# Eighteen product matmuls walk their columns in plain order, and nine separate contiguous matmuls are taken out

## The chip, the cores and the metric

The kernel runs on one core of a Trainium2 chip. The metric is the device time of one execution in microseconds. TensorE does the matrix products, VectorE, ScalarE and GpSimd the elementwise work, and DMA queues bring the weights from HBM. In rows of the profile PE is TensorE's matmul, PEld its weight load, DVE is VectorE, ACT ScalarE, POOL GpSimd, SP the engine whose queue issues the weight loads.

## The reference, cut to what matters

One layer of a hybrid decoder on 256 prompt tokens and 8 x 8 sample tokens (320 columns in all), model width 2048, feed-forward width 5632, in float32:

```python
xn = rms_norm(x, g_mix)
z = xn @ w_in                        # [B | C | h | q | k | v | gate_conv | gate_attn]
u = c_gate * h_conv
conv_out, conv_state = short_conv(u, conv_prev, w_conv)
y_conv = (b_gate * conv_out) @ w_conv_out
attn = prompt_attention(...)         # or sample_attention, window 128, sinks
y_attn = attn @ w_attn_out
merged = sigmoid(gate_c) * y_conv + sigmoid(gate_a) * y_attn
h = x + merged @ w_o
hn = rms_norm(h, g_ffn)
h = h + (silu(hn @ w_gate) * (hn @ w_up)) @ w_down
```

The output is the final norm of h, the last keys and values, and the convolution's state.

## The kernel before, in words

Activations lie with features on the 128 partitions and the 320 tokens along the free axis. Every float32 operand is held in two parts, hi and lo, in TensorE's rounded format, and a product of a weight block of 128 x 128 with the activations is three matmuls of 320 columns: hi x hi (pass 0), hi x lo (pass 1) and lo x hi (pass 2). `passes` (L150) orders them: passes 0 and 1 of a block follow one another and pass 2 comes some blocks later.

A product for 256 output features is `product` (L172): for each chunk of four blocks of 128 input features, `load_cols` (L132) issues the weights' DMA on SP's queue, ACT rounds them to `whi` (L129), DVE takes the rest as `wlo` (L130), and TensorE runs 24 matmuls of 320 columns (L186). Keys and values have a loop of their own, `kv_product` (L346, matmul at L372), whose chunks are four of one block and then six of two. The layer's order is: kv, q, then four times C, H, B, then eight times gc, ga, yc, ya, then eight wo (L186 each), then two halves of gate and up products (fg, fu) with the down product (dn, L997 to L1005) behind each half.

An activation row of 320 columns is stored as five pieces of 64 columns, 1040 elements apart for `xh`, `xl`, `hh` and `hl`. A product's matmul reads it, and writes its PSUM tile, in the order of `turns` (L101): four columns of piece 0, four of piece 1, and so on to piece 4, then the next four of each. The weights are read in plain order.

Between the chunks, `tick` (L145) advances a generator of side work: attention. Its matmuls stand on TensorE between chunks of C, H and B: eight visits for the prompt's scores (`prompt_scores`, L551, tiles `ps`), two for its values (`po`, L629), one for the sample's scores (`pss`, L689) and one for its values (`spo`, L753 and L763). In the first gate product's wake, two matmuls with ones (L211) give the second norm.

At nine places the kernel before has an additional matmul, `nudge` (L205). Its output is a scratch PSUM tile that nobody reads; it multiplies 320 neighbouring columns of `xh` (or `hh`) with 128 neighbouring columns of `xl` (or `hl`), in plain order:

```python
def nudge(rows, weights, n=T):
    x, w = (bass.AP(r.tensor, r.offset, [list(r.ap[0]), [1, m]]) for r, m in ((rows(0), n), (weights(0), P)))
    nc.tensor.matmul(ps_aux(u("nudge"))[:, :n], w, x, start=True, stop=True)
```

The places are: ahead of block 6 of kv; ahead of the third q product; behind the last of the eight visits of the prompt's scores; behind both visits of its values; behind the sample's scores; behind the sample's values; and ahead of the first up product of each half.

Of the kernel before, what the change touches and what calls it, by code (L numbers as in the profile page):

```python
# [17 lines left out]
T = TP + NB * TS  # L18
# [8 lines left out]
P = 128  # L27
# [25 lines left out]
def hybrid_layer(ctx: ExitStack, tc: tile.TileContext, a: dict, o: list):  # L53
    nc = tc.nc
# [17 lines left out]
    def ps_aux(name):  # L72
        return aux[0].tile([P, 512], F32, tag="aux", name=name)
# [3 lines left out]
    def u(s):  # L77
        uid[0] += 1
        return f"{s}_{uid[0]}"
# [21 lines left out]
    def turns(ap):  # L101

        return ap.rearrange("p s (i b) -> p i s b", b=4)

    def fives(ap):

        return ap.rearrange("p (s j) -> p s j", s=NS)
# [24 lines left out]
    def load_cols(w, k0, n, c0, behind=()):  # L132
# [4 lines left out]
            split_to(hi[:, :n, :], lo[:, :n, :], raw[:, :n, :])  # L137
        return hi, lo

    mark = {}  # L140
    side_work = [None]
    pending = []
    last = {}
# [28 lines left out]
    def product(load, nk, xh, xl, name, tiles=None, loaded=None):  # L172

        ps = [ps_acc(u(name)) for _ in range(2)]
        k0 = 0
        for n in tiles or [min(KT, nk - k) for k in range(0, nk, KT)]:
            hi, lo = load(k0, n)
            if loaded:
                loaded()
            order = [(k, c) for k in range(n) for c in range(2)]  # L180
            if k0 + n == nk:
                order.sort(key=lambda kc: kc[1])
            for k, c, i in passes(order, k0 + n == nk):
                kc = k0 + k
                w, x = ((hi, xh), (hi, xl), (lo, xh))[i]
                last["mm"] = nc.tensor.matmul(  # L186
                    turns(fives(ps[c][:, :T])), w[:, k, c * P:(c + 1) * P], turns(x(kc)),
                    start=(kc == 0 and i == 0), stop=(kc == nk - 1 and i == 2),
                )
            k0 += n  # L190
            while pending:
                with after(last["lo"], last["mm"]):
                    pending.pop(0)()
            tick()
        return ps

    def two_parts(src, tags=("ta", "tb")):
# [3 lines left out]
        nc.scalar.activation(hi, src, AF.Copy)  # L201
        nc.vector.tensor_sub(lo, src, hi.bitcast(F32))
        return hi, lo

    def nudge(rows, weights, n=T):  # L205
        x, w = (bass.AP(r.tensor, r.offset, [list(r.ap[0]), [1, m]]) for r, m in ((rows(0), n), (weights(0), P)))
        nc.tensor.matmul(ps_aux(u("nudge"))[:, :n], w, x, start=True, stop=True)

    def over_partitions(out, parts):
        for i, x in enumerate(parts):  # L210
# [48 lines left out]
    xh, xl = row_tiles(xp, ("xh_t", "xl_t"), KC, LEAD_X, ("xh", "xl"))  # L259
# [26 lines left out]
    def x_load(i, eng=nc.sync):  # L286
# [11 lines left out]
        out=ident, in_=ident, compare_op=ALU.not_equal, fill=1.0, base=0, pattern=[[-1, P]],  # L298
# [47 lines left out]
    def kv_product(tiles, x_after):  # L346

        ps = [ps_acc(u("kv")) for _ in range(4)]
        k0 = 0
        x_prep(0)  # L350
        for i, n in enumerate(tiles):
            if k0 == 6:
                nudge(xh, xl)
            hi, lo = load_kv(k0, n)
            if i == 0:
                x_prep(1)
            for b in x_after.get(i, ()):
                x_load(b)
            order = [(k, c) for k in range(n) for c in range(4)]
            if k0 + n == KC:  # L360
                order.sort(key=lambda kc: kc[1])
            seq = passes(order, k0 + n == KC)
            if i == 0:
                seq.sort(key=lambda kcm: kcm[2])
            for k, c, m in seq:
                kc = k0 + k
                if k0 and (k, c, m) == (0, 3 if n > 1 else 1, 0) and k0 + n < KC:
                    for kk in range(tiles[i + 1]):
                        x_prep(k0 + n + kk)
                    tick()  # L370
                w, x = ((hi, xh), (hi, xl), (lo, xh))[m]
                last["mm"] = nc.tensor.matmul(  # L372
                    turns(fives(ps[c][:, :T])), w[:, k, c * P:(c + 1) * P], turns(x(kc)),
                    start=(kc == 0 and m == 0), stop=(kc == KC - 1 and m == 2),
                )
            k0 += n
            if i == 0:
                tick()
        return ps
# [88 lines left out]
    def at_rows(part):  # L468
# [15 lines left out]
        out=sides[:, 0], in_=sides[:, 0], compare_op=ALU.is_ge, fill=0.0, base=-1, pattern=[[-1, WIN]],  # L484
# [158 lines left out]
    def prompt_attention():  # L643
        units = [(j * 2 + par, gp) for j in range(2) for gp in range(2) for par in range(2)]
        bias, sc, sm, turned, pts = {}, {}, {}, {}, {}
        bias[0] = bias_load(*units[0])
        for i in range(len(units) + 3):
            if i < len(units):
                if i + 1 < len(units):
                    bias[i + 1] = bias_load(*units[i + 1])  # L650
                sc[i] = prompt_scores(*units[i], bias.pop(i))
                if i + 1 == len(units):
                    nudge(xh, xl)
                yield
                sm[i] = prompt_softmax(*units[i], sc[i])
            if 0 <= i - 3 < len(units):
                pts[i - 3] = prompt_sides(i - 3, turned.pop(i - 3))
            yield
            if i >= 4 and i % 4 == 2:
                for n in (i - 5, i - 3):  # L660
                    kv, gp = units[n]
                    prompt_pv(kv // 2, gp, (pts.pop(n - 1), pts.pop(n)))
                nudge(xh, xl)
            if 0 <= i - 1 < len(units):
                turned[i - 1] = prompt_norm(i - 1, sc.pop(i - 1), *sm.pop(i - 1))
            yield
# [3 lines left out]
    def sample_attention(sm):  # L670
# [10 lines left out]
        for base in range(0, NB, 3):  # L681
            ps = ps_aux(u("pss"))
            n = min(3, NB - base)
            for b in range(base, base + n):
                o0 = (b - base) * W2
                for kv in range(NKV):
                    j, par = kv // 2, kv % 2
                    rows = slice(par * 64, par * 64 + 64)
                    nc.tensor.matmul(  # L689
                        ps[kv * 32:(kv + 1) * 32, o0:o0 + W2], qs[rows, j, b, :], kf[rows, b, j, :],  # L690
                        start=True, stop=True,
# [2 lines left out]
                s[:, base:base + n, :], ps[:, 0:n * W2].rearrange("p (b k) -> p b k", b=n),  # L694
                flip(bias_s).unsqueeze(1).to_broadcast([P, n, W2]),
            )
        nudge(xh, xl)
        yield
        yield

# [49 lines left out]
        for j in range(2):  # L750
            for par in range(2):
# [4 lines left out]
                    start=True, stop=False,  # L756
                )
        for b in range(NB):
            cv = cvs.pop(b)
            for j in range(2):  # L760
                for par in range(2):
# [3 lines left out]
                        cv[:, kv * HD:(kv + 1) * HD], ptw[:, kv, b * 32:(b + 1) * 32],  # L765
                        start=False, stop=(b == NB - 1),
                    )
        nudge(xh, xl)
        yield
        for j in range(2):  # L770
            src = pos[j][:, 0:256].rearrange("p (b g t) -> p g b t", b=NB, g=GRP)
            o = LEAD_A + j * 4 * at_row
            rows = at_t[:, o:o + 4 * at_row].rearrange("p (g w) -> p g w", g=GRP)[:, :, -2 * JS:]
# [42 lines left out]
    for j in range(2):  # L816
        for gp in range(2):
            if (j, gp) == (1, 0):
                nudge(xh, xl)
            ps = in_pair(O_Q + (j * 2 + gp) * CW, "q")  # L820
            pending.append(lambda j=j, gp=gp, ps=ps: q_out(j, gp, ps))
    side_work[0] = attention()
# [2 lines left out]
    for cp in range(4):  # L825
        c_sb = []
        ps = in_pair(O_C + cp * CW, "C")
# [4 lines left out]
        ps = in_pair(O_H + cp * CW, "H")  # L832
        conv = []
        for c in range(2):
# [13 lines left out]
            n = UL - 2  # L848
# [10 lines left out]
        ps = in_pair(O_B + cp * CW, "B")  # L859
# [17 lines left out]
    mm = mp_.enter_context(tc.tile_pool(name="mm", bufs=1, side="right"))  # L877
# [9 lines left out]
    for mp in range(8):  # L887
        c0 = mp * CW
        sg = {}
        for nm, off, tag in (("gc", O_GC, "ta"), ("ga", O_GA, "tb")):  # L890
            ps = in_pair(off + c0, nm)
# [5 lines left out]
        ps = product(  # L897
            lambda k0, n: load_cols(w_co, k0, n, c0), 8,
            cv_h, cv_l, "yc",
        )  # L900
# [126 lines left out]
    for half in range(2):  # L1027
# [4 lines left out]
        for fpair in range(nf // 2):  # L1032
            c0 = (f0 + fpair * 2) * P
            psg = product(
                lambda k0, n: load_cols(w_g, k0, n, c0), KC,
                hh, hl, "fg",
            )
            if half == 0 and fpair == 0:
                pss = ps_aux("pss2")
                over_partitions(pss[:, :T], two_parts(hacc, ("tc", "td")))  # L1040
                rstd_of(pss[:, :T], [P, T], "r2", hp, out=rb2)
            gs = []
            for c in range(2):
                t, t2 = tmp("ta", "gs")[:, :T], tmp("tb", "sg")[:, :T]
                nc.vector.tensor_mul(t, psg[c][:, :T], rb2)
                last["sig"] = nc.scalar.activation(t2, t, AF.Sigmoid)
                nc.vector.tensor_mul(t, t, t2)
                nc.vector.tensor_mul(t, t, rb2)
                gs.append(t)
            if fpair == 0:  # L1050
                nudge(hh, hl)
            psu = product(
                lambda k0, n: load_cols(w_u, k0, n, c0), KC,
                hh, hl, "fu",
            )
            for c in range(2):
                nc.vector.tensor_mul(gs[c], psu[c][:, :T], gs[c])
                f = fpair * 2 + c
                (first, rest), row = parts_of(gs[c]), a_move(f)
                nc.scalar.activation(row[:, :, JR:JT], rest, AF.Copy)  # L1060
                last["hi"] = nc.scalar.activation(row[:, :, 0:JR], first, AF.Copy)
                nc.vector.tensor_sub(row[:, :, JT:], rest, row[:, :, JR:JT].bitcast(F32))
                last["lo"] = nc.vector.tensor_sub(placed(a_low(f)), first, row[:, :, 0:JR].bitcast(F32))
                if half == 1:
                    nc.scalar.activation(a_first(f), gs[c][:, 0:P], AF.Copy)
# [258 lines left out]
```

## Time and profile before

| what | value |
|---|---|
| time, median of 3 runs | 1593.38 us (1593.12 to 1593.64) |
| time of the profiled execution | 1593.85 us |
| its span, first to last instruction | 1592.1 us |
| PE busy | 1583.2 us (99% of the span), 10899 matmuls |
| PEld busy | 1547.1 us (97%) |
| DVE busy | 890.9 us (56%) |
| ACT busy | 645.9 us (41%) |
| POOL busy | 133.2 us (8%) |
| granted TensorE clock | 0.998 of full speed on average |

The span lies within the profiled execution's time with 1.75 us around it. Matmuls are pipelined: the profile gives a 320-column matmul some 0.30 us, while the next one starts about 0.14 us after it, so the busy share says only that TensorE always has one under way. What a matmul costs the kernel is the distance from its start to the next one's start.

### The profile page before, as it was taken

To read this page: it belongs to the slowest core of one execution; us is meant where nothing else is said; L and a number is where in the kernel's file an instruction comes from. 1 tells how busy PE (TensorE), PEld (TensorE's weight loads), DVE (VectorE), ACT (ScalarE), POOL (GpSimd) and SP (SyncE) were. 2 spreads that over 40 slices of the span, in tenths; PEclk is the share of its full clock that TensorE was granted. 3 is DMA by queue.
4 is the path that set the end of the run, shared out by engine and by line. 5 is a ranking of instruction groups with operands and counts; after the bars stand their busy time and mean duration, and the time that the engine had idled before them with its cause. 6 is when DMAs were issued, how large, how long until landed. Compare 5 with 4: busy or idle time off the path is not lost.

```text
span 1592.1 us, 26453 instructions
## 1 busy us (share of the span) xinstructions
PE 1583.2 (99%) x10899; PEld 1547.1 (97%) x10899; DVE 890.9 (56%) x1314; ACT 645.9 (41%) x917; POOL 133.2 (8%) x213
## 2 busy tenths in 40 slices
PE   9999999999999999999999999999999999999998
PEld 9999999999999999999999999998888999999887
DVE  7879765445555445556555555553444455555556
ACT  7554443333333333344333333333333334444443
POOL 1414332000000003320000000000000000000021
PEclk9999999999999999999999999999999999999999
DMA  7757566544455544455554545555555454445663
GB/s 271 207 182 218 171 211 203 166 154 155 157 159 159 159 156 155 155 158 159 157 154 155 159 158 159 159 156 161 155 155 157 157 159 158 156 155 157 190 180 131
DMA packets 77648, 266.06 MB, mean 167 GB/s; under 512 B 9832, under 2 KB 13112, under 8 KB 77400
## 3 DMA queue, kind: packets, MB, share of 16 engines
q1 hardware_dynamic: 71736, 249.99, 50.2%
q0 software_dynamic: 5360, 13.84, 3.0%
q8 instruction: 85, 1.39, 0.4%
q10 hardware_dynamic: 432, 0.56, 0.1%
q14 instruction: 35, 0.29, 0.1%
HBM read 257.27 MB, written 9.04 MB: 167 GB/s over the span
## 4 chain that ended last, share of the span: by engine, by line
PE 99%; DMA 0%; DVE 0%; ACT 0%; issue 0%; SPq 0%; DVEq 0%
PE fu L186 19%; PE fg L186 19%; PE dn L997 9%; PE wo L186 7%; PE gc L186 7%; PE ga L186 7%; PE dn L1005 6%; PE C L186 3%; PE B L186 3%; PE H L186 3%; PE q L186 3%; PE ya L186 3%; PE yc L186 3%; PE dl L1001 2%; PE kv L372 2%; PE dn L1162 1%
## 5 line engine op out<-in xcount | busy, mean ns | idle before, releaser
L130 DVE TENSOR_TENSOR wlo<-wraw,whi 128x1024 fp32r<-128x1024 f32 (+1 forms) x460 | 563.1, 1225 | 564.5 <-ACT whi L129 453.4
L129 ACT ACTIVATE whi<-wraw 128x1024 fp32r<-128x1024 f32 (+1 forms) x460 | 485.5, 1056 | 722.0 <-PE fu L186 129.5
L186 PE MATMUL fu<-hh_t,whi 128*128 128x320 f32 x704 | 205.0, 301 | 0.0
L186 PE MATMUL fu<-hl_t,whi 128*128 128x320 f32 x704 | 205.0, 301 | 0.0
L186 PE MATMUL fg<-hh_t,whi 128*128 128x320 f32 x704 | 205.0, 301 | 0.0
L186 PE MATMUL fg<-hl_t,whi 128*128 128x320 f32 x704 | 205.0, 301 | 0.0
L186 PE MATMUL fu<-hh_t,wlo 128*128 128x320 f32 x704 | 158.8, 301 | 0.0
L186 PE MATMUL fg<-hh_t,wlo 128*128 128x320 f32 x704 | 158.8, 301 | 0.0
L997 PE MATMUL dn<-a_t,whi 128*128 128x512 f32 x640 | 155.2, 382 | 0.0
L186 PEld LDWEIGHTS fu<-hh_t,whi 128*128 128x128 f32 x704 | 131.7, 187 | 0.0
L186 PEld LDWEIGHTS fu<-hl_t,whi 128*128 128x128 f32 x704 | 131.7, 187 | 0.0
L186 PEld LDWEIGHTS fg<-hh_t,whi 128*128 128x128 f32 x704 | 131.7, 187 | 0.0
L186 PEld LDWEIGHTS fg<-hl_t,whi 128*128 128x128 f32 x704 | 131.7, 187 | 0.0
L997 PEld LDWEIGHTS dn<-a_t,whi 128*128 128x128 f32 x640 | 115.4, 187 | 16.5 <-issue 1.2
L186 PEld LDWEIGHTS fg<-hh_t,wlo 128*128 128x128 f32 x704 | 116.1, 187 | 0.0
L186 PEld LDWEIGHTS fu<-hh_t,wlo 128*128 128x128 f32 x704 | 116.1, 187 | 0.0
L1005 PEld LDWEIGHTS dn<-a_t,wlo 128*128 128x128 f32 x640 | 97.7, 188 | 6.9
L1005 PE MATMUL dn<-a_t,wlo 128*128 128x320 f32 x640 | 103.4, 301 | 0.0
L186 PE MATMUL gc<-xh_t,whi 128*128 128x320 f32 x256 | 74.5, 301 | 0.0
L186 PE MATMUL gc<-xl_t,whi 128*128 128x320 f32 x256 | 74.5, 301 | 0.0
L186 PE MATMUL ga<-xh_t,whi 128*128 128x320 f32 x256 | 74.5, 301 | 0.0
L186 PE MATMUL ga<-xl_t,whi 128*128 128x320 f32 x256 | 74.5, 301 | 0.0
(317 smaller groups left out, 2695.7 us busy)
## 6 DMA issues: line engine op xcount, KB each, us to landing
wraw<-in_w_in_dram SPq DMA_DIRECT2D x128, 512.0 KB, 3.9
wraw<-in_w_gate_dram SPq DMA_DIRECT2D x88, 512.0 KB, 3.8
wraw<-in_w_up_dram SPq DMA_DIRECT2D x88, 512.0 KB, 3.7
wraw<-in_w_down_dram SPq DMA_DIRECT2D x88, 512.0 KB, 3.7
wraw<-in_w_o_dram SPq DMA_DIRECT2D x32, 512.0 KB, 3.8
wraw<-in_w_conv_out_dram SPq DMA_DIRECT2D x16, 512.0 KB, 3.6
wraw<-in_w_attn_out_dram SPq DMA_DIRECT2D x16, 512.0 KB, 3.7
wraw<-in_w_kv_dram SPq DMA_DIRECT2D x6, 512.0 KB, 7.5
```

Source lines behind the costliest of these rows:

```text
L129: last["hi"] = nc.scalar.activation(hi, src, AF.Copy)
L130: last["lo"] = nc.vector.tensor_sub(lo, src, hi.bitcast(F32))
L186: last["mm"] = nc.tensor.matmul(turns(fives(ps[c][:, :T])), w[:, k, c * P:(c + 1) * P], turns(x(kc)), start=(kc == 0 and i == 0), stop=(kc ...
L372: last["mm"] = nc.tensor.matmul(turns(fives(ps[c][:, :T])), w[:, k, c * P:(c + 1) * P], turns(x(kc)), start=(kc == 0 and m == 0), stop=(kc ...
L997: nc.tensor.matmul(turns(placed(ps[c])), parts[k][0][:, cs], turns(a_move(k)), start=k == 0, stop=False)
L1001: nc.tensor.matmul(low, a_low(k), parts[k][0], start=k == 0, stop=k == nf - 1 and c0 < E0)
L1005: last["mm"] = nc.tensor.matmul(turns(placed(ps[c])[:, :, 0:JT]), parts[k][1][:, cs], turns(a_move(k)[:, :, 0:JT]), start=False, stop=k == ...
L1162: nc.tensor.matmul(turns(placed(ps[c])[:, :, JR:]), held[k][0][:, cs], turns(a_move(k)[:, :, JR:]), start=k == 0, stop=k == nf - 1,)
```

## The change

`nudge` no longer issues a matmul. It sets a flag, and the next matmul of a product (now through `weigh`, shared by `product` and `kv_product`) leaves out `turns` on both its output and its activations: it walks the five pieces of 64 columns one after the other, writing 320 neighbouring PSUM columns. Its data and its result are the same. The nine places keep the call; there are nine new ones: ahead of blocks 1 and 4 of kv, and behind the seven other visits of the prompt's scores.

```diff
+    plain = [False]
+
+    def weigh(out, w, x, **kw):
+        walk = (lambda ap: ap) if plain[0] else turns
+        plain[0] = False
+        last["mm"] = nc.tensor.matmul(walk(fives(out)), w, walk(x), **kw)
+
+    def nudge():
+        plain[0] = True
...
-                last["mm"] = nc.tensor.matmul(
-                    turns(fives(ps[c][:, :T])), w[:, k, c * P:(c + 1) * P], turns(x(kc)),
+                weigh(
+                    ps[c][:, :T], w[:, k, c * P:(c + 1) * P], x(kc),
                     start=(kc == 0 and i == 0), stop=(kc == nk - 1 and i == 2),
                 )
...
-    def nudge(rows, weights, n=T):
-        x, w = (bass.AP(r.tensor, r.offset, [list(r.ap[0]), [1, m]]) for r, m in ((rows(0), n), (weights(0), P)))
-        nc.tensor.matmul(ps_aux(u("nudge"))[:, :n], w, x, start=True, stop=True)
...
-            if k0 == 6:
-                nudge(xh, xl)
+            if k0 in (1, 4, 6):
+                nudge()
...
                 sc[i] = prompt_scores(*units[i], bias.pop(i))
-                if i + 1 == len(units):
-                    nudge(xh, xl)
+                nudge()
                 yield
...
                     prompt_pv(kv // 2, gp, (pts.pop(n - 1), pts.pop(n)))
-                nudge(xh, xl)
+                nudge()
```

The remaining four calls change in the same way. On the built program's TensorE queue the change is these eighteen matmuls and nothing else.

Here is the queue before, at the first visit of the prompt's scores (`ps`) in the midst of a C product:

```order
L562 MATMUL ps_135_1180<-k_498,at_t 128x256 x2
L565 MATMUL ps_136_1181<-k_498,at_t 128x256
L186 MATMUL C_1129<-xh_t,whi_1195 128x16x5x4
L186 MATMUL C_1129<-xl_t,whi_1195 128x16x5x4
L186 MATMUL C_1130<-xh_t,whi_1195 128x16x5x4
```

And the same place after the change:

```order
L568 MATMUL ps_133_1176<-k_496,at_t 128x256 x2
L571 MATMUL ps_134_1177<-k_496,at_t 128x256
L145 MATMUL C_1125<-xh_t,whi_1191 128x320
L145 MATMUL C_1125<-xl_t,whi_1191 128x16x5x4
L145 MATMUL C_1126<-xh_t,whi_1191 128x16x5x4
```

No instruction is added there; the first C matmul behind the scores has lost its walk in turns (16x5x4) and goes through 320 columns in plain order.

This is the queue before, behind the sample's values (`spo`) in the last B product:

```order
L763 MATMUL spo_3181<-ptw,cv_2819 64x32 x2
L207 MATMUL nudge_3218<-xh_t,xl_t 128x320
L186 MATMUL B_3148<-xh_t,whi_3222 128x16x5x4
L186 MATMUL B_3148<-xl_t,whi_3222 128x16x5x4
L186 MATMUL B_3149<-xh_t,whi_3222 128x16x5x4
```

And after the change:

```order
L768 MATMUL spo_3169<-ptw,cv_2807 64x32 x2
L145 MATMUL B_3136<-xh_t,whi_3208 128x320
L145 MATMUL B_3136<-xl_t,whi_3208 128x16x5x4
L145 MATMUL B_3137<-xh_t,whi_3208 128x16x5x4
```

One matmul fewer stands there, and the first matmul of the product has the plain order that the nudge had.

Last, the queue before at the first up product (`fu`), behind the two matmuls with ones that end in the tile `pss`:

```order
L211 MATMUL pss_7677<-part_7679,ones_r 128x320
L207 MATMUL nudge_7705<-hh_t,hl_t 128x320
L186 MATMUL fu_7707<-hh_t,whi_7711 128x16x5x4
L186 MATMUL fu_7707<-hl_t,whi_7711 128x16x5x4
```

And after the change:

```order
L217 MATMUL pss_7663<-part_7665,ones_r 128x320
L145 MATMUL fu_7691<-hh_t,whi_7695 128x320
L145 MATMUL fu_7691<-hl_t,whi_7695 128x16x5x4
L145 MATMUL fu_7692<-hh_t,whi_7695 128x16x5x4
```

Again the separate matmul is gone, and the product's own first matmul is the plain one.

## Rows read from the trace of the kernel before

**Rows 1.** The page: the chain that ended last, shares of the span.

```profile
PE 99%; DMA 0%; DVE 0%; ACT 0%; issue 0%; SPq 0%; DVEq 0%
```

**Rows 2.** All waits of PE (us in total, times, longest).

```profile
PE wm L305 <- PEq L1304: 0.8, 1, 0.8
PE kv L372 <- ACT whi L129: 0.6, 1, 0.6
```

**Rows 3.** The chain in order of time: start us, us, what.

```profile
91.66 10.24 PE C L186 x72
102.62 10.10 PE H L186 x72
...
589.43 107.52 PE wo L186 x768
```

**Rows 4.** Timeline of PE at the last scores' visit: start us, us, what.

```profile
170.38 0.31 PE L207 MATMUL nudge<-xh_t,xl_t 128*128 128x320 f32 x1
170.53 0.31 PE L186 MATMUL B<-xh_t,whi 128*128 128x320 f32 x1
...
171.52 0.30 PE L186 MATMUL B<-xl_t,whi 128*128 128x320 f32 x1
```

**Rows 5.** Timeline of PE behind the sample's scores.

```profile
216.04 0.41 PE L207 MATMUL nudge<-xh_t,xl_t 128*128 128x320 f32 x1
216.29 0.30 PE L186 MATMUL B<-xh_t,whi 128*128 128x320 f32 x1
```

**Rows 6.** Timeline of PE in kv, with idle time and its releaser.

```profile
7.20 0.42 PE L372 MATMUL kv<-xh_t,whi 128*128 128x320 f32 x1 [0.60 <-ACT whi L129]
7.45 0.30 PE L372 MATMUL kv<-xl_t,whi 128*128 128x320 f32 x1
...
15.84 0.31 PE L207 MATMUL nudge<-xh_t,xl_t 128*128 128x320 f32 x1
```

**Rows 7.** Timeline of all engines in kv: the whi of blocks 1 and 3 to 5.

```profile
6.52 0.63 ACT L129 ACTIVATE whi<-first_w 128x512 fp32r<-128x512 f32 x1 [1.19 <-DMA first_w<-in_w_kv_dram]
...
11.18 1.15 ACT L129 ACTIVATE whi<-wraw 128x512 fp32r<-128x512 f32 x2
12.43 0.30 PE L372 MATMUL kv<-xh_t,whi 128*128 128x320 f32 x1
```

**Rows 8.** Timeline of PE at the second scores' visit.

```profile
102.45 0.31 PE L186 MATMUL H<-xh_t,whi 128*128 128x320 f32 x1
102.60 0.31 PE L186 MATMUL H<-xl_t,whi 128*128 128x320 f32 x1
102.75 0.30 PE L186 MATMUL H<-xh_t,whi 128*128 128x320 f32 x1
```

**Rows 9.** The chain around the end of the first down product and behind it.

```profile
1257.74 1.76 PE dn L997 x8
1259.50 0.46 PE rowacc L1001 x2
...
1261.08 13.46 PE fg L186 x96
1274.54 0.15 PE nudge L207
```

**Rows 10.** Timeline of DVE and PE before the last H chunk.

```profile
244.79 1.22 DVE L743 TENSOR_TENSOR ptn<-pns,blk 64x1024 f32<-64x1024 f32 x1 [6.37 <-DMA pns<-scr]
245.94 2.35 DVE L130 TENSOR_TENSOR wlo<-wraw,whi 128x1024 fp32r<-128x1024 f32 x2
247.67 0.72 PE L186 MATMUL H<-xh_t,wlo 128*128 128x320 f32 x4
```

**Rows 11.** The chain behind the sample's values, and of the first half's products.

```profile
256.77 10.10 PE B L186 x72
...
696.95 13.44 PE fg L186 x96
...
1060.29 13.44 PE fu L186 x96
```

More of the change, by code (lines that the diff above doesn't have):

```diff
@@ L371, in kv_product @@
                 w, x = ((hi, xh), (hi, xl), (lo, xh))[m]
-                last["mm"] = nc.tensor.matmul(
-                    turns(fives(ps[c][:, :T])), w[:, k, c * P:(c + 1) * P], turns(x(kc)),
+                weigh(
+                    ps[c][:, :T], w[:, k, c * P:(c + 1) * P], x(kc),
                     start=(kc == 0 and m == 0), stop=(kc == KC - 1 and m == 2),
@@ L696, in sample_attention @@
             )
-        nudge(xh, xl)
+        nudge()
         yield
@@ L767, in sample_attention @@
                     )
-        nudge(xh, xl)
+        nudge()
         yield
@@ L818, in hybrid_layer @@
             if (j, gp) == (1, 0):
-                nudge(xh, xl)
+                nudge()
             ps = in_pair(O_Q + (j * 2 + gp) * CW, "q")
@@ L1050, in hybrid_layer @@
             if fpair == 0:
-                nudge(hh, hl)
+                nudge()
             psu = product(
```

## The prediction

> **What bounds the kernel now.** I read the page's shares first, then the waits of PE, then the chain in order of time, and last the timeline at each place that the diff touches. The reader should see in the first that nothing but TensorE is on the chain: 99% of the span [rows 1]. The waits say the same: TensorE waits twice in 1592 us, 1.4 us together, both in the first 8 us [rows 2]. So every nanosecond between two matmul starts is kernel time, and an extra matmul is hidden by nothing.
>
> The chain then shows that this distance has two values for the same instruction. The eight wo products run 768 matmuls in 107.52 us, 140.0 ns each. The 72 matmuls of C behind the first visit of the prompt's scores take 10.24 us, 142.2 ns each, and the 72 of H behind the second visit 10.10 us, 140.3 ns [rows 3]. Nothing waits in either; the work is the same. I call the two the fast step and the slow step; they differ by 2.2 ns. In the trace the step is chosen at an interruption and kept until the next one. Slow are the kv matmuls from 7.45 us to the nudge at 15.84 us (59 in 8.39 us, 142.2 ns each) [rows 6] and that one C stretch. All else in turned order runs at 140, behind all nine nudges too. Nearly nothing is left to win in the step itself.
>
> **What is removed: nine nudges.** At the last scores' visit the nudge starts at 170.38 and the product at 170.53; the eight distances from the nudge to 171.52 add up to 1.14 us, that is eight fast steps (1.12) and 0.02 us of settling [rows 4]. Taking out the nudge while the next matmul settles in the same way removes one ordinary step, 0.14 us. Four of the nine stand behind attention matmuls of other tile shapes, and there the nudge is followed by a distance of 0.25 us (216.04 to 216.29) [rows 5]. That is not the nudge's price: the first kv matmul after a wait, a turned one of the product, has the same 0.25 us behind it (7.20 to 7.45) [rows 6]. Whatever matmul comes first pays it, so here, too, one ordinary step goes. Nine steps of 0.140 are **1.26 us**; between 9 x 0.12, if a plain first matmul settles 0.02 longer than a nudge, and 9 x 0.15, the nudge's distance in rows 4, it is 1.08 to 1.35.
>
> **What is added: the plain order of eighteen product matmuls.** No product matmul of the trace walks in plain order through five pieces, so its price is bounded. From below: 0.14 us, the turned one, no extra. From above: the plain 512-column matmuls at the end of the down product take 0.23 us each (two in 0.46), the turned ones of the same width 0.22 (eight in 1.76), so 0.01 us more; the nudge's 0.15 against 0.14 [rows 4, 9] is also 0.01. I take 0.01, within the 0.02 us of settling counted above. At the nine old places it is already in the nudge's settling. Far off stands 0.11 us, what the 0.25 us restart has over a step [rows 6]; no plain matmul inside a stream of its own tile shape paid that.
>
> The page "Advanced Engine Details and Errata" of the Trainium skill, section PSUM Cachelines, says that any non-contiguous access pattern slows matmuls significantly. By that the turned product would be the slow one and the eighteen plain ones at least as quick; at nothing extra for any of the eighteen the sum would gain 18 x 0.01 = 0.18 us at most, an estimate. The traces disagree with it: runs of four columns step at 140 ns, and contiguous nudges and contiguous rowacc matmuls need some 10 ns more.
>
> **The six visits that already recover.** Behind the second visit the first H matmuls are 0.15 us apart, twice [rows 8], some 0.02 us of settling, with no nudge there, and the stretch is fast. A plain matmul there buys nothing and may add up to 0.02; six times 0 to 0.02, I take a loss of **0.05**.
>
> **The first visit.** If the plain matmul brings the fast step, 72 x 2.2 ns = 0.16 us, less 0.03 of settling: a gain of **0.13**; if it doesn't, a loss of 0.02.
>
> **Keys and values.** 59 x 2.2 ns = 0.13 us less two settlings of 0.025 would be 0.08. But here TensorE follows ACT closely. At block 1 whi ends at 7.15 (6.52 + 0.63) and PE starts at 7.20, so the hand-over takes 0.05; at block 4 whi ends at 12.33 and PE starts at 12.43, so 0.05 is spare [rows 7]. The 36 matmuls ahead of it gain 36 x 2.2 = 0.08 less 0.025, just that. If TensorE has to wait, it pays the restart of 0.11 and gains nothing from the first part; behind it the plain matmul of block 4 gives 24 x 2.2 = 0.05. I take a gain of **0.04**, between a loss of 0.09 and a gain of 0.13.
>
> **Nothing else moves**: ACT, POOL and SP keep their order, and on DVE one 128x4 addition of a softmax goes behind a weight part. Weight parts are released by TensorE's own progress, so they move up with it. The tightest place further on is an H chunk: DVE waits 6.37 us for a DMA of the sample's attention, and of its two weight parts from 245.94 the first, done near 247.12 (half of 2.35 later), is read at 247.67, so 0.55 is spare [rows 10]. By then TensorE would be 0.96 us earlier (six nudges 0.84, the first visit 0.13, kv 0.04, less 0.05). The DMA starts behind DVE work that is itself marked by TensorE's matmuls, so it should move along; were it fixed, the wait would be 0.41 and a restart 0.11, 0.5 in all.
>
> **The sum.** 1.26 + 0.13 + 0.04 - 0.05 = 1.38 us. The profiled execution took 1593.85, so 1592.47 of its own time. It is 0.47 above the median of the runs, 1593.38; the prediction of the median is **1592.0**, 0.09% faster. With the bounds added up (1.08 - 0.02 - 0.09 - 0.12 - 0.5 = 0.35, and 1.35 + 0.16 + 0.13 = 1.64) the case spans 1591.7 to 1593.0. A measurement of this kernel can tell about 0.2% from no change, that is 1590.2 to 1596.6, and this whole case lies inside.
>
> **Rivals.**
>
> *The plain product does not set the fast step where it must hold longest (slower).* Behind the sample's values, 72 B, eight times gc, ga, yc, ya, all wo and the first fg follow with no other interruption: 72 + 2304 + 768 + 96 = 3240 matmuls [rows 11]. Slow, they cost 3240 x 2.2 ns = 7.1 us: 1599.1. The first half has 28 products fg and fu, 13.44 us each from 696.95 to 1073.73 [rows 11]; 27 of them stand behind the matmuls with ones, 2592 matmuls, 5.7 us: 1597.7. It decides from about 2100 slow matmuls on, 4.6 us, which brings 1592.0 to 1596.6. For it: kv's second chunk, a turned start from a restart, fell into the slow step, and the spot behind the sample's values is such a restart; the nudge read one run of 320 columns and wrote a bank of its own, the plain product reads five runs and adds into the bank that the next matmul uses. Against it: the first fg behind the down product has 13.46 us for 96, 140.2 ns each, with no nudge ahead [rows 9], and six of seven visits without any nudge recovered. Chance 0.12.
>
> *The change doesn't pay: the saved steps are given back.* The plain products cost more than 0.01, or waits in kv and at the H chunk take it, or short stretches between visits (24 to 96 matmuls each) go slow at 0.05 to 0.2 us. At 0.08 us more for each of the eighteen nothing is left: 1593.0 to 1594. For it: 0.05 and 0.55 us of spare time; against it, the plain rows at hand. Chance 0.08.
>
> *Only the stretch of the second half is slow.* Behind its nudge at 1274.54 [rows 9] stand 15 products, 1440 matmuls, 3.2 us: 1595.2, within 0.2%. Chance 0.02.
>
> *More than the sum.* Nothing off the sum is slow, and the bounds end at 1.64, while 0.2% is 3.2 us. Chance 0.02.
>
> **How the numbers follow.** The forecast has 0.76, the rivals 0.12, 0.08, 0.02 and 0.02. Faster by over 0.2% is 0.02; slower by over 0.2% is 0.12; the rest, 0.86, is within. The range 1591.4 to 1595.3 holds the forecast's bounds, the change that doesn't pay and the slow second half, 0.86; the long slow stretches are left out. The likeliest case's own range is 1591.7 to 1593.0.
>
> **What would show it.** Right: no nudge row, the chain's wo still 768 in 107.52, the C stretch behind the first visit near 10.10, kv from block 1 to block 6 near 0.06 us shorter, and the first B behind the sample's scores followed after 0.25 us, then by steps of 0.14. Wrong: a wo or fu row of the chain at 142.2 ns for each matmul, a wait of PE at L145 behind whi or wlo, or plain matmuls with 0.2 us and more behind them in the midst of a stream.

## The result and the profile after

The change made the kernel slower: 1600.56 us (median of 6 runs, 1600.15 to 1600.75) against 1593.32 (6 runs, 1593.12 to 1593.64), a ratio of 1.0045 with a 95% interval of 1.0032 to 1.0058. The forecast was 1592.0 with a range up to 1595.3; the time is 1.5 us above the rival in which the stream behind the sample's values goes slow (1599.1).

The chain of the changed kernel, in order of time (start us, us, engine, tile, line, count), answers to [rows 3, 11]:

```profile
91.13 10.26 PE C L145 x72
102.10 10.24 PE H L145 x72
113.05 3.38 PE H L145 x24
...
256.31 10.44 PE B L145 x72
266.75 13.65 PE gc L145 x96
...
594.43 109.23 PE wo L145 x768
703.65 13.65 PE fg L145 x96
717.60 13.45 PE fu L145 x96
```

The reader should see where the time is. wo takes 109.23 us for 768 matmuls, 142.2 ns each, where it took 107.52, and gc and fg 13.65 for 96 instead of 13.44: everything from the sample's values to the first up product goes in the slow step. From 717 us on, fu is back at 13.45. TensorE's clock is not the reason. For the same window of the two traces, first the kernel before and then the changed one, these rows give the stretch, its length, PE's busy time with the number of matmuls, the granted clock, the DMA share and GB/s:

```profile
266.00:589.00 323.00, 323.00 (x2310) 1.00 0.51 160
266.00:589.00 323.00, 323.00 (x2273) 1.00 0.51 158
```

The granted clock is 1.00, the level of 2.4 GHz, in both, and 37 matmuls fewer fit into the same time. The place where the slow stretch begins and the one where it ends, on the timeline of PE in the changed kernel (start us, us):

```profile
256.24 0.41 PE L145 MATMUL B<-xh_t,whi 128*128 128x320 f32 x1
256.49 0.31 PE L145 MATMUL B<-xl_t,whi 128*128 128x320 f32 x1
...
717.15 0.45 PE L217 MATMUL pss<-part,ones_r 128*128 128x320 f32 x2
717.44 0.31 PE L145 MATMUL fu<-hh_t,whi 128*128 128x320 f32 x1
```

And the same two places before:

```profile
256.36 0.41 PE L207 MATMUL nudge<-xh_t,xl_t 128*128 128x320 f32 x1
...
710.53 0.31 PE L207 MATMUL nudge<-hh_t,hl_t 128*128 128x320 f32 x1
710.67 0.31 PE L186 MATMUL fu<-hh_t,whi 128*128 128x320 f32 x1
```

From the plain B at 256.24 to the plain fu at 717.44 are 461.20 us. Before, from the nudge at 256.36 to the first fu at 710.67 are 454.31 us, with one step more in it: 6.89 us lost net, 7.03 without the step saved. Everything behind it is equal (1592.1 - 710.67 = 881.4 and 1598.7 - 717.44 = 881.3), and what stands ahead of it is 0.12 us shorter. The slow stretch is thus the whole of the loss between the two traces. Ahead of it savings and other losses nearly cancel: H behind the second visit, for one, takes 10.24, before 10.10.

PE waits nowhere for data in the changed kernel, and no instruction was added; the loss is in the distance between matmuls that have all they need. Its one wait is at the start:

```profile
PE wm L311 <- PEq L1309: 0.8, 1, 0.8
```

### The profile page after: what moved, and what is told of

Its sections match the earlier page's. It is cut to its first block, busy times and chain, and to the rows that moved or that the text cites. A ratio compares the mean times of both kernels' runs of the same rounds, so it can differ in the third digit from the quotient of the medians.

```text
span 1598.7 us, 26435 instructions
## 1 busy us (share of the span) xinstructions
PE 1590.6 (99%) x10890; PEld 1554.9 (97%) x10890; DVE 890.4 (56%) x1314; ACT 646.6 (40%) x917; POOL 133.7 (8%) x213
## 4 chain that ended last, share of the span: by engine, by line
PE 99%; DVE 0%; issue 0%; DVEq 0%; ACT 0%
PE fg L145 19%; PE fu L145 18%; PE dn L1002 9%; PE ga L145 7%; PE gc L145 7%; PE wo L145 7%; PE dn L1010 6%; PE B L145 3%; PE ya L145 3%; PE yc L145 3%; PE C L145 3%; PE H L145 3%; PE q L145 3%; PE dl L1006 2%; PE kv L145 2%; PE dn L1167 1%
## 5 line engine op out<-in xcount | busy, mean ns | idle before, releaser
L145 PE MATMUL wo<-m_h,whi 128*128 128x320 f32 x256 | 75.6, 304 | 0.0
```

The costliest lines, as they stand in the source:

```text
L145: last["mm"] = nc.tensor.matmul(walk(fives(out)), w, walk(x), **kw)
```

## The experiments

Of every kernel I read the chain's wo row, which tells the step behind the sample's values (107.52 fast, 109.23 slow), and the first distances at the places.

**1. The old matmul back at one place.** In the changed kernel `push` is the old separate matmul:

```diff
-        nudge()          # behind the sample's values
+        push(xh, xl)
```

> The changed kernel with the old separate contiguous matmul put back at one place, behind the sample's values, instead of the plain product there. Theory A (the plain product fails to set the fast step at that place, and the 3240 matmuls behind it are slow): gc, ga, yc, ya and wo return to 140.0 ns, wo 107.5 us for 768, and the time is 1600.6 - 7.1 + 0.1 = 1593.6 us; the scores' visits stay as they are in the changed kernel. Rival B (the stream arrives there in another state because of the slow visits upstream, and nothing at this one place would help): wo stays at 109.2 us, the time at 1600.7.

Measured: 1593.46 us (ratio to before 1.0001, 0.9991 to 1.0010), wo 107.52. This one place is the loss, and what goes wrong upstream doesn't reach past it. Six of the eight visits' stretches were still slow, as in the change.

**2 and 3. Nothing there, and the plain matmul alone.** Both start from the kernel before and touch this place only.

```diff
 # experiment 2
-        nudge(xh, xl)    # behind the sample's values
 # experiment 3
-        nudge(xh, xl)    # behind the sample's values
+        plain[0] = True  # the next product matmul is plain, as in the change
```

> The kernel before without its separate matmul behind the sample's values, and with no plain product in its place. Theory A (left alone, the restart there falls into the slow step, as in the second chunk of keys and values): 1593.3 - 0.1 + 7.1 = 1600.3 us, wo 109.2. Rival C (the separate matmul was never needed there; it is the plain product that brings the slow step): 1593.2 us, wo 107.5.

> The kernel before with one part of the change alone: behind the sample's values the separate matmul is replaced by a plain-order first product matmul; the other eight separate matmuls stay. Theory A: the 3240 matmuls behind it are slow, 1600.3 us, wo 109.2. Rival B (upstream state): fast, 1593.2 us, wo 107.5.

Measured: 2 took 1593.15 us (0.9999, 0.9989 to 1.0010), wo 107.52; 3 took 1606.31 us (1.0082, 1.0067 to 1.0097), wo 109.23. Theory A was wrong in 2: a bare turned start was fast here, so the separate matmul was not what held the fast step, and with the plain product matmul in its place the slow one came. Experiment 3 is slower than the change itself, since its slow stream also runs on behind the separate matmul at the first up product. Its chain there:

```profile
703.33 13.65 PE fg L145 x96
716.99 0.29 PE pss L218 x2
717.28 0.14 PE nudge L214
717.42 13.65 PE fu L145 x96
731.08 13.65 PE fg L145 x96
```

In the changed kernel a slow stream met the plain product matmul at the same place and left it fast (13.45). The separate matmul is no surer there: in 10 (below) the slow stream stays slow behind it, as here, and in 9 (below) it becomes fast (fu at 717.50, 13.45). So neither kind of matmul is a dependable reset.

**4. One plain matmul more, in mid-stream.**

```diff
     for mp in range(8):
         c0 = mp * CW
         sg = {}
+        if mp == 0:
+            nudge()
```

> The changed kernel with one more plain-order product matmul, the first of the first gc product, 72 matmuls behind the sample's values, in the midst of a slow stream. If a plain product sets the fast step in mid-stream and fails only at the restart behind attention matmuls (theory A1): from there fast, 1600.6 - 3168 x 2.2 ns = 1593.6 us, wo 107.5. If a plain product never sets it out of a slow stream (theory A2): 1600.6 us, wo 109.2.

Measured: 1593.12 us (0.9999, 0.9988 to 1.0009). Its chain:

```profile
256.57 10.44 PE B L145 x72
267.01 13.45 PE gc L145 x96
...
589.59 107.52 PE wo L145 x768
```

B is slow (10.44, as in the change), and from the plain matmul in gc on all is fast: theory A1. At this place a plain product matmul sets the fast step in a slow stream that already runs, with no interruption near it.

**5. A candidate: turned visits and values.** In the changed kernel, no plain matmul behind the values and behind seven visits, the old separate matmul behind the eighth.

```diff
-                nudge()
+                if i + 1 == len(units):
+                    push(xh, xl)
...
-        nudge()          # behind the sample's values
```

> A candidate: the changed kernel with nothing behind the sample's values (turned first product matmul), the seven visits of the scores without a separate matmul left in turned order, and the old separate matmul behind the eighth visit; plain products stay in keys and values, ahead of the third q, behind both prompt values, behind the sample's scores and ahead of both first ups. Theory P (at an interruption whatever stands there only shifts how the stream arrives; turned there is fast at the values and at six of seven visits, plain is fast at the places that stay): eight separate matmuls less, 8 x 0.14 = 1.1, and 0.1 in keys and values: 1593.3 - 1.2 = 1592.1 us, wo 107.5, only the C stretch of the first visit slow. Rival (plain products in turned surroundings cost more than the trace shows): 1593.3 or more.

Measured: 1592.63 us in the profiled execution, 1599.31 to 1599.58 in the four others (median of all five 1599.46; 1.0038, 1.0024 to 1.0052). The profiled one is 0.8 us below the 1593.44 of the kernel before, of 1.2 forecast. The 6.9 us between the two times are the size of one slow stretch behind the values; of the four others there is no trace, and that the fast one is just the profiled one leaves open whether profiling itself shifted it. In the profiled one the tight H chunk [rows 10] is late, as this timeline of DVE and PE shows:

```profile
244.34 1.22 DVE L753 TENSOR_TENSOR ptn<-pns,blk 64x1024 f32<-64x1024 f32 x1 [6.81 <-DMA pns<-scr]
245.48 3.48 DVE L130 TENSOR_TENSOR wlo<-wraw,whi 128x1024 fp32r<-128x1024 f32 x3
...
246.77 0.81 PE L145 MATMUL H<-xh_t,wlo 128*128 128x320 f32 x4
247.42 0.30 PE L145 MATMUL H<-xh_t,whi 128*128 128x320 f32 x1
```

Four matmuls at wlo take 0.65 us up to the next start where 0.56 are four steps: 0.09 late, behind the DMA.

**6. The plain walk one matmul later.** The changed kernel; behind the values the first matmul is turned and the second plain.

```diff
-        walk = (lambda ap: ap) if plain[0] else turns
-        plain[0] = False
+        walk = (lambda ap: ap) if plain[0] == 1 else turns
+        plain[0] = max(0, plain[0] - 1)
...
-        nudge()          # behind the sample's values
+        plain[0] = 2
```

> The changed kernel, but behind the sample's values the second product matmul is the plain one and the first is turned. Theory P: no rule says which step this gives; the walk alone, moved by one matmul, can change it. Rival Q (any plain product matmul close behind the values' restart puts the stream into the slow step): 1600.6 us, wo 109.2. Rival R (a plain matmul in a running stream sets the fast step, it fails only as the first behind a restart): 1593.5 us, wo 107.5.

Measured: 1592.75 us (8 runs, 1592.59 to 1593.16; 0.9996, 0.9986 to 1.0006), wo 107.52, and the 72 B behind the values take 10.30, in the change 10.44. That is what rival R says, but this kernel was not run with a turned start alone at the values, which was fast in 2: what the plain second matmul adds is not separated here. The timeline of PE has no pause behind the second matmul, the plain one; the step itself is told by the chain's row.

```profile
255.77 0.42 PE L145 MATMUL B<-xh_t,whi 128*128 128x320 f32 x1
256.02 0.31 PE L145 MATMUL B<-xl_t,whi 128*128 128x320 f32 x1
256.18 0.30 PE L145 MATMUL B<-xh_t,whi 128*128 128x320 f32 x1
```

```profile
255.84 10.30 PE B L145 x72
```

**7, 9 and 10. What of the first plain matmul is it?** All three start from the kernel before and touch the values only. In 7 the separate matmul walks five runs; in 9 it is a copy of the product's first matmul in plain order, into a scratch tile, with the product whole and turned behind it; in 10 the product's first matmul is plain and its second and third are exchanged.

```diff
 # experiment 7
+        nc.tensor.matmul(fives(ps_aux(u("five"))[:, :T]), w, xh(0), start=True, stop=True)
 # experiment 9, in weigh
+            nc.tensor.matmul(fives(ps_aux(u("dup"))[:, :T]), w, x, start=True, stop=True)
 # experiment 10, in product
+            if plain[0]:
+                seq[1], seq[2] = seq[2], seq[1]
```

> The kernel before, with the separate matmul behind the sample's values reading a product's activations in plain order, five runs of 64 columns 1040 apart, in place of 320 neighbouring columns; its output stays a scratch tile. If reading five runs is what brings the slow step: 1593.3 + 7.1 = 1600.4 us, wo 109.2. If it is that the plain matmul belongs to the product (its bank, its weights, one instruction fewer): 1593.3 us, wo 107.5.

> The kernel before; behind the sample's values the separate matmul is a copy of the product's first one (its weights, its activations in plain order) into a scratch tile, and the product follows whole and in turned order. If the plain walk over the product's own data brings the slow step: 1600.4 us or more, wo 109.2. If it is what follows (the turned stream then starts with its second matmul, not with its first): 1593.3 us, wo 107.5.

> The kernel before with the plain first product matmul behind the sample's values alone, and with its second and third matmul exchanged, so that the plain one is followed by a matmul into the other PSUM bank with other weights. If two matmuls in a row into one bank (the plain one and a turned one behind it) bring the slow step: fast now, 1593.2 us. If only the arrival in time counts: no bank matters, slow as without the exchange, 1606.3 us, or 1600.3 if the first up stream recovers.

Measured: 7 took 1593.85 us (1.0001, 0.9991 to 1.0011), 9 took 1600.42 (1.0043, 1.0028 to 1.0058), 10 took 1606.34 (1.0080, 1.0062 to 1.0098). So it is not the reading of five runs as such (7), not two matmuls in a row into one bank (10), and not that an instruction is missing (9). The separate matmuls of 7 and 9 have the same walk and differ in their operands: block 0 of xh with weights from xl in 7, block 4 of xh with the product's own whi in 9. Their timelines start alike, from 7 and then from 9:

```profile
256.39 0.41 PE L770 MATMUL five<-xh_t,xl_t 128*128 128x320 f32 x1
256.65 0.30 PE L186 MATMUL B<-xh_t,whi 128*128 128x320 f32 x1
```

```profile
255.84 0.41 PE L144 MATMUL dup<-xh_t,whi 128*128 128x320 f32 x1
256.09 0.31 PE L147 MATMUL B<-xh_t,whi 128*128 128x320 f32 x1
```

The restart is 0.26 us in the fast one and 0.25 in the slow one, a difference of the size of the rows' rounding; what decides is not seen in these rows.

**8. All nine separate matmuls out**, every product turned.

```diff
-        nc.tensor.matmul(ps_aux(u("nudge"))[:, :n], w, x, start=True, stop=True)
+        return
```

> The kernel before with all nine separate matmuls taken out and every product in turned order. If most places take the fast step by themselves, as the values do: 1593.3 - 1.3 + 0.4 (keys and values up to 39 us) + 0.4 (behind the eighth visit) = 1592.8 us. If the first up stream goes slow without its separate matmul, 5.7 more: 1598.5 us, and fu and fg from 710 us at 13.65 us for 96.

Measured: 1600.34 us (1.0044, 1.0030 to 1.0059). Both readings missed: it was slow behind the values (wo 109.23), where the turned start of 2 had been fast, and fast from the first up on. It was slow behind the sample's scores already (C and H there 13.65 each for 96, before 13.44).

**11 and 14. The turned start behind the values.** 11 is the candidate of 5 with `ptn`, the DVE instruction that waits for the DMA, one chunk later; 14 is 11 with a separate matmul behind the sample's scores, in place of the plain product matmul there.

```diff
 # experiment 11: ahead of ptn, and one fewer behind it
+        yield
 # experiment 14: behind the sample's scores
-        nudge()
+        push(xh, xl)
```

> The candidate with turned visits (times of 1592.6 and 1599.5 in different executions), with the sample's probabilities taken up one chunk later on DVE, so that two weight parts are no longer queued behind an instruction that waits for a DMA. If that wait (DVE 6.8 us for the probabilities' DMA, PE 0.08 late at an H chunk, then slow up to the values) decides which step the stream takes behind the values: all executions fast, 1592.4 us, no distance over 0.2 us within H. If the turned start behind the values is undecided by itself: both times again.

> The kernel with the probabilities taken up later (turned start behind the sample's values, slow in five of five executions, 1599.6 us), with one separate matmul more, behind the sample's scores, 40 us ahead of the values. It shifts the scratch PSUM banks of the sample's values by one, to those of the kernel in which a turned start there was fast. If the bank decides: 1592.8 us, wo 107.5. If not: 1599.8 us, wo 109.2.

Measured: 11 took 1599.63 us in all five executions (1599.41 to 1599.74; 1.0038, 1.0025 to 1.0050), with no wait in H and a fast stream up to the values; 14 took 1592.59 (8 runs, 1592.28 to 1592.96; 0.9994, 0.9984 to 1.0004). My reading of 5 fell: the late H chunk is not what makes the start behind the values slow. The step there went with an edit 40 us upstream. That 14 shifts the scratch banks was my reason for it; it also adds a matmul, turns the product matmul behind it and moves every later one by 0.14 us, and these were not separated. Nor was chance: the two ran on different chips, and 5 showed both times in one kernel.

**12 and 13. Plain as the second matmul.** 12 is a mixture: second at the first and eighth visit and at the values, turned at the other visits, first elsewhere, `ptn` later. 13 is the change with the counter of 6 in `weigh` and this line in `nudge`: at all eighteen places the plain matmul is the second.

```diff
 def nudge():
-    plain[0] = True
+    plain[0] = 2
```

> A candidate: plain product matmuls and no separate ones; behind the first and the eighth visit of the scores and behind the sample's values it is the second product matmul that is plain, at the other places the first as in the change; visits two to seven turned; the sample's probabilities taken up one chunk later. If a plain matmul inside a running stream sets the fast step: 1593.4 - 9 x 0.14 - 0.1 (keys and values) - 0.1 (first visit) = 1591.9 us, wo 107.5, the first visit's C near 10.1 us. If it is worth nothing there, the first and eighth visits' stretches stay slow (264 x 2.2 = 0.6): 1592.4 us.

> The change as it stands, but at all eighteen places the second product matmul is the plain one and the first stays turned. Theory R (a plain matmul with a product matmul ahead of it sets the fast step; as the first behind attention it is a matter of luck): all eight visits' stretches, both stretches behind the prompt's values, and all behind the sample's values run at 140 ns, wo 107.5; 1593.4 - 1.26 - 0.1 - 0.16 + 0.1 = 1592.0 us. Rival P (the walk only shifts the arrival, any place can land in either step): some of the eighteen stretches at 142.2 ns; if the one behind the sample's values, 1599 us.

Measured: 12 took 1592.10 us (11 runs, 1591.60 to 1592.61; 0.9991, 0.9982 to 1.0000), 13 took 1592.13 (11 runs, 1591.53 to 1592.69; 0.9990, 0.9981 to 0.9999), beside 1593.54 for the kernel before on the same chips. In 12 the second visit, a turned start, was slow (H 10.24), where before it was fast. The chain of 13:

```profile
91.04 10.09 PE C L145 x72
101.83 10.09 PE H L145 x72
112.63 3.37 PE H L145 x24
...
169.56 6.73 PE B L145 x48
176.29 13.44 PE C L145 x96
...
245.44 1.22 DVE wlo L130
246.71 2.53 PE H L145 x16
...
255.60 10.30 PE B L145 x72
265.90 13.44 PE gc L145 x96
...
588.46 107.52 PE wo L145 x768
```

All eight visits' stretches and all behind the values are fast, where the change had six visits and the values slow and the kernel before one visit. The tight H chunk does bind here: DVE's wlo is on the chain.

```profile
246.71 0.85 PE L145 MATMUL H<-xh_t,wlo 128*128 128x320 f32 x4 [0.27 <-DVE wlo L130]
```

## Why the prediction was wrong, point by point

**What bounds the kernel** held: TensorE alone, and two steps of 140.0 and 142.2 ns, each kept over long stretches. Most of the result is 3240 matmuls that changed from one to the other. That the step changes only at an interruption did not hold: in 4 a plain product matmul changed it in mid-stream.

**The step that failed** is in the part on the nine nudges: "Taking out the nudge while the next matmul settles in the same way removes one ordinary step". At the values the next matmul did not settle in the same way. Having shown that all nine places were fast behind a nudge, I carried that over to a plain product matmul; no row showed one as the first behind attention. In all four kernels with such a matmul at the values (the change, 3, 4 and 10) the slow step followed, in 9 behind a separate copy of it too, while in 2, which differs from 3 in this alone, a bare turned start was fast. Since bare turned starts took either step in other kernels (8, 11), it is not shown that the plain walk as such decides, and not the arrival that it shifts.

**The rival** had the right place and price, 7.1 us against 7.03 measured, at a chance of 0.12. Its reasons were wrong: not the five runs (7), not the bank (10), and not a fast step that only the nudge could set (2). The evidence that I set against it, turned starts that recovered, says nothing of plain ones. A price of 7.1 us beside a gain of 1.3 should also have stood in the range, which ended at 1595.3.

**The six visits** were put at a loss of 0.05 us for settling. Measured: of the seven visits that got a new plain matmul, the first stayed slow (10.26, forecast 10.1) and of the six that recovered four turned slow (the second, fourth, fifth and seventh), and so did the eighth, whose nudge was replaced. With the values' stretch aside, 456 matmuls more are slow than before (72 + 72 + 72 + 48 + 192), 1.0 us at 2.2 ns. That is most of the 1.5 us by which the time exceeds the rival's. It is the same failed step.

**Nine steps of 0.14** fit the runs where the step stayed fast: 13, which differs from the change only in which matmul is plain, is 1.41 us below its own kernel before, where 1.38 was forecast for the change. The sum came out so; single terms are not told apart, since the interval reaches from 0.2 to 3.0 us and 13 has a wait that the forecast did not have. Nor do the starts of the first C stretch show them: 91.13 in the change and 91.66 before [rows 3], but from 91.05 (2) to 91.70 (7) in the six traces that are alike up to the values (before, 2, 3, 7, 9, 10).

**Keys and values** rested on a slow stretch that belongs to one execution. In 2, whose kv matmuls and nudge are those of the kernel before, the same 59 matmuls go from 6.96 to 15.22, 8.26 us or 140.0 ns each, where [rows 6] has 8.39:

```profile
6.96 0.30 PE L372 MATMUL kv<-xl_t,whi 128*128 128x320 f32 x1
...
15.22 0.31 PE L207 MATMUL nudge<-xh_t,xl_t 128*128 128x320 f32 x1
```

There was no wait for ACT in 2, and no restart with it. So nothing of the 0.04 can be counted on, and the same instructions take either step.

**The price of a plain matmul** in a running stream was right: C in 13 takes 10.09 us for 72 with a plain second matmul, where the all-turned H of the kernel before takes 10.10 [rows 3], so the difference is within the rows' rounding.

**The tight H chunk** was right as a risk, not as a term: the changed kernel did not wait there, 1 and 13 did, 0.21 and 0.27 us (bound 0.5).

**What stays open**: why a first plain matmul behind attention lands in the slow step at the values and at six visits but not at the two others, behind the prompt's values or the sample's scores, and why a bare turned start behind the values was fast in 2 and 14, slow in 8 and 11, and both in 5. It went with the operands (7 against 9) and with an edit 40 us upstream (11 against 14), each seen in one pair of kernels; the mechanism below that was not found. That a plain matmul with a product matmul ahead of it sets the fast step is a count, not an explanation: the gc of 4, the values of 6, three places of 12 and all eighteen of 13, with no counterexample. Such a place weighs most where a slow stream is seen ahead of it. That is so at the gc of 4, and twice in kv: in the traces of 1 and 14 the 23 matmuls ahead of block 6 take 3.28 and 3.27 us (142.6 and 142.2 ns each), and from 20 matmuls behind the plain one there on, 24 take 3.36 (140.0). Next come the starts of 13 that were slow in another kernel: the first visit, slow before and in the change, and the values and five visits, slow in the change.

## What to carry to other kernels

Where one engine issues thousands of alike instructions back to back, read the distance from start to start, stretch by stretch: two values for the same instruction mean a state that a small edit can flip, and its price is the length of the stretch behind the edit, not the size of the edit. Of an edit at such a place ask what it can undo as well as what it saves, and time each place alone. Here a matmul meant to settle a stream worked, as far as it was tried, once the stream ran, one matmul behind the restart.

## What the runs showed of the hardware

The same matmuls of 320 columns run 140.0 or 142.2 ns apart at a granted clock of 0.998 to 0.999 in every kernel, and of 1.00 in both of the windows compared above, without any wait, over up to 3240 matmuls, and nothing in the waits or the busy shares tells the two apart. "TensorE: Matmul & The Clock Gate" of the Trainium skill, section "Wait — 56ns, not 53.3ns?", gives N / 2.4 GHz and about 2.5 ns between the starts of matmuls of N columns, which makes 135.8 ns for 320 columns, an estimate from that page. Both measured steps lie above it, and the traces decide.

The same instructions can take either step in different executions: the kv matmuls of the kernel before and of 2 (142.2 and 140.0 ns), and by its times the kernel of 5 (1592.6 in the profiled one and 1599.5 us). So a median of a few runs of such a kernel can hide a second time.

"Advanced Engine Details and Errata" of the Trainium skill, section PSUM Cachelines, says that any non-contiguous pattern slows matmuls significantly, and asks that every two consecutive elements be contiguous, which runs of four columns meet. The traces do not bear out the first: turned walks of four columns step at 140.0 ns, and a stretch of 72 takes 10.09 us with a plain second matmul (13) and 10.10 without one. No run here tests the second.
